# A two-layer trunk in fp32 on one core: the gate/up products at the entry of each FFN, one pair of tiles done with eight products, three pairs led, norms ahead of weights

## The chip, the core and the metric

The kernel runs on one core of a Trainium2 chip. The metric is device time of one execution in microseconds (us), as the median of several executions. Everything is computed for one sequence of 512 tokens by 1024 channels, in fp32.

## What is computed

The reference is a trunk of two layers. Each layer has a mixer and a SwiGLU FFN, and each of these sub-layers stands between two RMS norms:

```python
for layer in range(DEPTH):                      # 2
    h = rmsnorm(x, mix_pre_g[layer])
    m = even_mixer(h, ...) if layer % 2 == 0 else odd_mixer(h, ...)
    x = x + rmsnorm(m, mix_post_g[layer])
    h = rmsnorm(x, ffn_pre_g[layer])
    x = x + rmsnorm(swiglu(h, ffn_w_gate[layer], ffn_w_up[layer], ffn_w_down[layer]), ffn_post_g[layer])

def swiglu(h, w_gate, w_up, w_down):            # 512x1024 -> 512x2816 -> 512x1024
    return (jax.nn.silu(h @ w_gate) * (h @ w_up)) @ w_down
```

The change lies in the two norms ahead of `swiglu` and in its two products `h @ w_gate` and `h @ w_up`.

## The kernel before

Every fp32 product is made of three matmuls on rounded operands: each operand is split into a high and a low part, and `mm3` (L134 to L138) issues high by high (L136), low by high (L137) and high by low (L138). A split costs a cast on ACT (the high part) and a subtraction on DVE (the low part). For weights this is `split_weights`: `whi` on ACT at L158, `wlo` on DVE, which all DVE instructions record as L100 because they go through one helper.

**The gate/up products.** The 22 tiles of the hidden width are done as NP = 11 pairs of a gate and an up tile. The token axis and the contraction axis are both halved, so that a pair is a 2 by 2 block product. It is done with seven half-size products instead of eight, in the manner of Strassen and Winograd: two straight ones, A11 and A12 (tokens of blocks 0 and 1 against the two halves of the channels), four with sums of token blocks, S1 to S4, against sums of weight blocks, and A22. `gate_product` is one of these: 24 matmuls of 128x128 by 128x256. Its weight is a unit of 512 KB, loaded by SP into one of RAW = 6 `raw` buffers, in places summed in place with another (`raw<-raw` on DVE, `add_to`), then split. `first` makes A11 of a pair and copies its bank aside (L867), `second` adds A12 and gates the result (`gated`: silu on ACT at L857, a multiplication by the up tile on DVE). The rest of the pair, in the loop at the end of `ffn`, needs S1 to S4 and A22.

**The lead.** The tokens come in four blocks of 128. Blocks 0 and 1 are normed first, and A11 and A12 need only those. So the first LEAD = 5 pairs do `first` and `second` ahead of everything else, while blocks 2 and 3 are still being normed and their sums S1 to S4 are made (`Blocks.put`). `need(2, 3)` then stands ahead of the loop over the pairs.

**The norms.** `Finish` is the end of a sub-layer: `half` squares a half of an output block on ACT (L705) and multiplies it by the gain on DVE; `block` takes 1/rms (an addition on DVE, a power on POOL at L636), adds into `xres` on DVE and squares again on ACT (L722); `second` makes the normed block `h` (two `tmp<-xres,small,gain` on DVE); `transpose` makes eight transposes of it on PE (L743); then `Blocks.put` splits and sums the transposed block (casts L660, copies L668 and L672 on ACT, the rest on DVE).

**The order.** Each engine works through its queue in order. A scheduler orders the instructions of all engines by priority as the code emits them; `tc.high_priority()` moves what stands in it ahead. In the kernel before that is the splitting and summing of weights. `later(d, f)` puts a step d us of modelled work behind the present place in the stream of matmuls; T1, T2 and T3 are such delays of the norm's steps. `gate_recipes` lists the loads, sums and splits of the weight units in the order in which `unit()` hands them out.

Of the kernel before, what the change touches and what calls it, by code (L numbers as in the profile page):

```python
# [10 lines left out]
AF = mybir.ActivationFunctionType  # L11
# [8 lines left out]
NB = T // P  # L20
# [1 line left out]
FT = FF // P  # L22
NP = FT // 2

LEAD = 5
RAW = 6

A11, A12, S1, S2, S3, S4, A22 = range(7)
EPS = 1e-6
WINDOWS = (2, 4, 8, 16)  # L30
OUT_ORDER = (0, 1, 2, 7, 6, 5, 3, 4)


WARM = 8
ON_DVE = (0, 2)
# [29 lines left out]
def tile_trunk(ctx: ExitStack, tc: tile.TileContext, cst_d, sh_d, xw_d, x_d, gains_d, pw_d, w_d, out_d):  # L65
# [88 lines left out]
        return raw[:, :n]  # L154

    def split_weights(raw, hi, lo):
        with tc.high_priority():
            nc.scalar.copy(out=hi, in_=raw)  # L158
            vec.tensor_sub(out=lo, in0=raw, in1=f32(hi))

    def add_to(acc, other, eng):
        with tc.high_priority():
            eng.tensor_add(out=acc, in0=acc, in1=other)


# [15 lines left out]
    def gate_recipes(first):  # L181

        def load(j, q):
            return rawtile(w_d[first + 4 * j + q])

        for j in range(LEAD):
            recipes.append(lambda j=j: load(j, 0))
            recipes.append(lambda j=j: load(j, 3))
        for j in range(NP):
            st = {}  # L190

            def p1(j=j, st=st):
                st["v"] = load(j, 0)
                return st["v"]

            def q5(j=j, st=st):
                if j < LEAD:
                    p1(j, st)
                st["12"] = load(j, 1)
                add_to(st["v"], st["12"], vec)  # L200
                return st["v"]

            def p6(j=j, st=st):
                st["22"] = load(j, 2)
                add_to(st["v"], st["22"], vec)
                return st["v"]

            def p2(j=j, st=st):
                st["21"] = load(j, 3)
                return st["21"]  # L210

            def p7(j=j, st=st):
                add_to(st["12"], st["22"], vec)
                return st["12"]

            def q4(j=j, st=st):
# [422 lines left out]
    class Plain:  # L639


        def put(self, i, tps):
            for hf, tp in enumerate(tps):
                tv = tp.rearrange("p (k t) -> p k t", k=4)
                ks = slice(4 * hf, 4 * hf + 4)
                nc.scalar.copy(out=hBh[:, i, ks], in_=tv)
                vec.tensor_sub(out=hBl[:, i, ks], in0=tv, in1=f32(hBh[:, i, ks]))

    class Blocks:


        def put(self, i, tps):
            cs = slice(i % 2 * P, i % 2 * P + P)

            def view(ap):
                return ap.rearrange("p (k t) -> p k t", k=4)
# [12 lines left out]
                return  # L669
            ta, tb = tmp(), tmp()  # L670
            x22, s1, s2, s3 = view(ta[:, :T]), view(ta[:, T:]), view(tb[:, :T]), view(tb[:, T:])
            nc.scalar.copy(out=x22, in_=tv[1])  # L672
            vec.tensor_sub(out=s1, in0=tv[0], in1=x22)
            split(S1, s1)
            vec.tensor_sub(out=s2, in0=s1, in1=x11)
# [2 lines left out]
            split(S3, s3)  # L678
            vec.tensor_add(out=s1, in0=s2, in1=x12)
            split(S4, s1)  # L680
            split(A22, x22)

    class Finish:

# [11 lines left out]
        def half(self, i, hf, acc, made_by=None):  # L696

            if i not in self.u:
                self.u[i] = (small(2), tmp())
            ss, u = self.u[i]  # L700
            cs = slice(hf * T, (hf + 1) * T)
            if made_by is not None:
                made_by(u[:, cs])
                acc = u[:, cs]
            nc.scalar.activation(out=junk[:, cs], in_=acc, func=AF.Square, scale=1.0 / 32, accum_out=ss[:, hf:hf + 1])  # L705
            vec.tensor_mul(out=u[:, cs], in0=acc, in1=self.gpost[:, cs])

        def block(self, i):
            ss, u = self.u.pop(i)
            gpre = self.gpre  # L710
            r = rstd(ss, 2)
# [14 lines left out]
            box = {}  # L726

            def second():
                r2 = rstd(s2, len(parts))
                h = box["h"] = tmp()  # L730
                for cs in halves:
                    vec.scalar_tensor_tensor(out=h[:, cs], in0=x[:, cs], scalar=r2, in1=gpre[:, cs],
                                                   op0=ALU.mult, op1=ALU.mult)
                later(T1 if i < NB - 1 else T2, transpose)

            def transpose():
                h = box["h"]
# [92 lines left out]
    def ffn(layer):  # L830
# [30 lines left out]
        def first(j):  # L861

            b1 = ps()
            gate_product(b1, unit(), A11)

            y = gs[NP - 1 - j][:, 1] if j < LEAD else ytile()
            nc.scalar.copy(out=y, in_=b1)  # L867
            return b1, y

        def second(j, b1):  # L870
            gate_product(b1, unit(), A12, True)
            gated(j, 0, b1, tmp()[:, :256])

        led = []
        need(0, 1)
        for j in range(LEAD):
            led.append(first(j))
            second(j, led[j][0])
        need(2, 3)
        for j in range(NP):  # L880
            b1, y = led[j] if j < LEAD else first(j)
            z, c = hx[:, j % 2, :T], hx[:, j % 2, T:]
            b3 = ps()
            gate_product(b3, unit(), S1)
# [233 lines left out]
```

## Time and profile before

| | |
|---|---|
| median of 3 runs | 1083.9 us (1083.37 to 1085.91) |
| the profiled execution | 1087.36 us |
| its span in the trace | 1085.6 us |
| PE busy | 1041.1 us (96%) |
| PE weight loads busy | 931.0 us (86%) |
| DVE busy | 768.8 us (71%) |
| ACT busy | 516.9 us (48%) |
| mean granted clock of PE | 0.988 |

PE is TensorE's matmuls, PEld its weight loads, which run beside them, DVE is VectorE, ACT ScalarE, POOL GpSimd, SP the queue that issues the loads. The busy time of PE is modelled from pipelined matmuls, so a busy PE is not PE at its peak. The two FFNs are called FFN 0 and FFN 1 below. The gate/up stage of FFN 0 runs from its first matmul on `hTh` at 196.74 us to the first matmul of the down product at 434.01 us, that of FFN 1 from 722.67 to 957.08 us.

### The profile page before, as it was taken

How to read it: one execution, taken by the hardware profiler on the slowest of the kernel's cores; microseconds unless marked ns; L12 is line 12 of the kernel's file. 1: busy time of each engine (PE TensorE's matmuls, PEld its weight loads, DVE VectorE, ACT ScalarE, POOL GpSimd, SP SyncE). 2: the span in 40 equal slices, each digit the busy share in tenths (PEclk: the TensorE clock that was granted, in tenths of full speed). 3: DMA queues.
4: the chain of work that ended last, by engine and by line, in shares of the span. 5: the costliest groups of instructions: out<-in, count | busy, mean ns of one | idle time of the engine just before them, and what ended most of it. 6: DMA issues, size and time to landing. Idle time of an engine off the chain costs nothing. (4 is left out here: it accounts for less than half of the span.)

```text
span 1085.6 us, 16315 instructions
## 1 busy us (share of the span) xinstructions
PE 1041.1 (96%) x6558; PEld 931.0 (86%) x6558; DVE 768.8 (71%) x1045; ACT 516.9 (48%) x815; POOL 60.7 (6%) x96
## 2 busy tenths in 40 slices
PE   8989999789999999999999999897999999999997
PEld 6867777789999999888898887687999999988886
DVE  3778875788998989432357589468899889963313
ACT  6747644654444446332245894355444444542301
POOL 0020100100000000000012102210000000000000
PEclk9989999899999999999999999998999999999999
DMA  8563353232443244334123234132442432443201
GB/s 320 170 146 83 107 171 120 98 114 101 156 131 104 80 139 131 113 108 150 57 75 101 84 110 152 26 115 97 148 141 101 129 105 80 136 135 98 98 1 77
DMA packets 36188, 125.08 MB, mean 115 GB/s; under 512 B 4368, under 2 KB 4368, under 8 KB 36112
## 3 DMA queue, kind: packets, MB, share of 16 engines
q1 hardware_dynamic: 35536, 121.94, 35.6%
q10 hardware_dynamic: 576, 2.10, 0.5%
q8 instruction: 51, 0.84, 0.3%
q14 instruction: 25, 0.20, 0.1%
HBM read 117.73 MB, written 2.10 MB: 110 GB/s over the span
## 5 line engine op out<-in xcount | busy, mean ns | idle before, releaser
L158 ACT CAST whi<-raw 128x1024 fp32r<-128x1024 f32 x230 | 239.0, 1047 | 310.4 <-PE ps L137 113.1
L100 DVE TENSOR_TENSOR wlo<-raw,whi 128x1024 fp32r<-128x1024 f32 (+1 forms) x238 | 286.3, 1212 | 124.7 <-ACT whi L158 119.6
L136 PE MATMUL ps<-hTh,whi 128*128 128x256 f32 (+1 forms) x960 | 294.6, 307 | 5.5 <-ACT whi L158 2.5
L138 PE MATMUL ps<-hTh,wlo 128*128 128x256 f32 (+1 forms) x960 | 294.0, 307 | 3.8 <-DVE wlo L100 3.8
L137 PE MATMUL ps<-hTl,whi 128*128 128x256 f32 (+1 forms) x960 | 292.2, 305 | 3.5 <-DVE hTl L100 3.5
L136 PEld LDWEIGHTS ps<-hTh,whi 128*128 128x128 f32 x960 | 182.7, 190 | 15.0 <-ACT whi L158 3.1
L138 PEld LDWEIGHTS ps<-hTh,wlo 128*128 128x128 f32 x960 | 182.4, 190 | 13.3 <-DVE wlo L100 4.6
L137 PEld LDWEIGHTS ps<-hTl,whi 128*128 128x128 f32 x960 | 182.8, 190 | 12.2 <-DVE hTl L100 3.7
L136 PE MATMUL ps<-up,whi 128*128 128x256 f32 x528 | 149.8, 284 | 2.2 <-DVE hx L100 2.1
L137 PE MATMUL ps<-up,whi 128*128 128x256 f32 x528 | 149.4, 283 | 0.0
L138 PE MATMUL ps<-up,wlo 128*128 128x256 f32 x528 | 149.2, 283 | 0.0
L100 DVE TENSOR_TENSOR raw<-raw 128x1024 f32<-128x1024 f32 x88 | 106.9, 1220 | 8.1 <-DMA raw<-in_w 7.8
L136 PEld LDWEIGHTS ps<-up,whi 128*128 128x128 f32 x528 | 101.1, 191 | 3.1 <-DVE hx L100 3.0
L137 PEld LDWEIGHTS ps<-up,whi 128*128 128x128 f32 x528 | 101.2, 192 | 0.0
L138 PEld LDWEIGHTS ps<-up,wlo 128*128 128x128 f32 x528 | 101.1, 192 | 0.0
L100 DVE TENSOR_TENSOR tmp<-ps,gain 128x512 f32<-128x512 f32 x32 | 21.9, 690 | 59.0 <-ACT junk L705 58.9
L636 POOL TENSOR_TENSOR small<-small,nhalf 128x1 f32<-128x1 f32 x28 | 15.4, 549 | 800.1 <-DVE small L100 800.1
L137 PE MATMUL ps<-wlo,hTh 128*128 128x512 f32 (+2 forms) x160 | 55.8, 352 | 3.2 <-DVE wlo L100 3.1
L138 PE MATMUL ps<-whi,hTl 128*128 128x512 f32 (+2 forms) x160 | 55.5, 350 | 0.0
L136 PE MATMUL ps<-whi,hTh 128*128 128x512 f32 (+2 forms) x160 | 54.3, 351 | 0.6 <-ACT whi L303 0.6
L705 ACT ACTIVATE junk<-ps 128x512 bf16<-128x512 f32 x32 | 19.0, 596 | 60.7 <-PE ps L138 60.2
L138 PE MATMUL ps<-whi,hTh 128*128 128x512 f32 x96 | 38.0, 396 | 0.0
(220 smaller groups left out, 1655.3 us busy)
## 6 DMA issues: line engine op xcount, KB each, us to landing
raw<-in_w SPq DMA_DIRECT2D x200, 512.0 KB, 3.8
gain<-in_gains SPq DMA_DIRECT2D x7, 512.0 KB, 4.2
raw<-in_xw SPq DMA_DIRECT2D x6, 516.0 KB, 9.1
big<-in_x ACTq DMA_DIRECT2D x4, 512.0 KB, 7.8
big<-big SPq DMA_DIRECT2D x16, 128.0 KB, 4.2
xres<-in_x SPq DMA_DIRECT2D x4, 512.0 KB, 5.0
out_dram<-xres SPq DMA_DIRECT2D x3, 512.0 KB, 2.6
big<-tmp SPq DMA_DIRECT2D x8, 128.0 KB, 3.9
```

The lines of the kernel that those rows point to most:

```text
L100: self.last = fn(*a, **k)
L136: nc.tensor.matmul(out, lhsT=ah, rhs=bh, start=start, stop=False, skip_group_check=more)
L137: nc.tensor.matmul(out, lhsT=ah, rhs=bl, start=False, stop=False, skip_group_check=more)
L138: nc.tensor.matmul(out, lhsT=al, rhs=bh, start=False, stop=stop, skip_group_check=more)
L158: nc.scalar.copy(out=hi, in_=raw)
L636: nc.gpsimd.tensor_tensor(out=r, in0=ms, in1=nhalf[:, :1], op=ALU.pow)
L705: nc.scalar.activation(out=junk[:, cs], in_=acc, func=AF.Square, scale=1.0 / 32, accum_out=ss[:, hf:hf + 1])
```

## The change

One pair (number 3, `WHOLE`) is done with all eight block products, A11, A12, A21 and A22, straight on the four quarters of its weights: each weight unit is used twice, and no weight sums, bank adds or copies are made for it. It comes right behind the leads, and the leads are three pairs instead of five. A21, the lower token half against the first half of the channels, is split straight from the transposes into a new slot, and A22 too, ahead of the sums. The norm's steps are issued in high priority, the weights' splits and sums in `high_priority(AHEAD)`, and the transposes of this norm 2.5 us of modelled work later.

```diff
-LEAD = 5
+LEAD = 3
+
+WHOLE = LEAD
...
+AHEAD = 1500
...
     def split_weights(raw, hi, lo):
-        with tc.high_priority():
+        with tc.high_priority(AHEAD):
...
     def add_to(acc, other, eng):
-        with tc.high_priority():
+        with tc.high_priority(AHEAD):
...
+        for q in (0, 3, 1, 2):
+            recipes.append(lambda q=q: load(WHOLE, q))
         for j in range(NP):
+            if j == WHOLE:
+                continue
...
     class Blocks:
...
+        delay = 2.5
...
+            split(A21, tv[0])
             nc.scalar.copy(out=x22, in_=tv[1])
+            split(A22, tv[1])
...
-            split(A22, x22)
...
-            nc.scalar.activation(out=junk[:, cs], in_=acc, func=AF.Square, scale=1.0 / 32, accum_out=ss[:, hf:hf + 1])
-            vec.tensor_mul(out=u[:, cs], in0=acc, in1=self.gpost[:, cs])
+            with tc.high_priority():
+                nc.scalar.activation(out=junk[:, cs], in_=acc, func=AF.Square, scale=1.0 / 32,
+                                     accum_out=ss[:, hf:hf + 1])
+                vec.tensor_mul(out=u[:, cs], in0=acc, in1=self.gpost[:, cs])
 
         def block(self, i):
+            with tc.high_priority():
+                self._block(i)
...
-                later(T1 if i < NB - 1 else T2, transpose)
+                later((T1 if i < NB - 1 else T2) + self.sink.delay, transpose)
...
         for j in range(LEAD):
-            led.append(first(j))
-            second(j, led[j][0])
-        need(2, 3)
+            b1 = first(j)
+
+            nc.scalar.copy(out=gs[NP - 1 - j][:, 1], in_=b1)
+            second(j, b1)
+        ws = [unit(), unit()]
+        for n in range(2):
+            for f, fs in ((2 * n, (A11, A12)), (2 * n + 1, (A21, A22))):
+                b = ps()
+                if f == 1:
+                    need(2, 3)
+                gate_product(b, ws[0], fs[0])
+                gate_product(b, ws[1], fs[1], True)
+                gated(WHOLE, f, b, tmp()[:, :256])
+            if n == 0:
+                ws = [unit(), unit()]
         for j in range(NP):
-            b1, y = led[j] if j < LEAD else first(j)
+            if j == WHOLE:
+                continue
```

Lines of the changed kernel are shifted: DVE's L100 is L104, `whi` L162, the squares L719 and L741, the transposes L763, the silu L877, the copy of a led bank L895.

How the order of work moves is shown at three places, all at the entry of FFN 0. The first is DVE, from the addition behind the square of block 2 to the normed block 3. In the rows `xres_1831` is block 2 of the stream, `xres_1833` block 3, `wlo` the low part of a weight, and `tmp<-xres,small,gain` the normed block `h`. Before:

```order
L100 TENSOR_SCALAR small_2108<-small_2077 128x1
L100 TENSOR_TENSOR tmp_2093<-ps_1948,gain_1823 128x512
L100 SCALAR_TENSOR_TENSOR tmp_2112<-xres_1831,small_2110,gain_1825 128x512
L100 TENSOR_TENSOR wlo_2205<-raw_2206,whi_2204 128x1024
L100 SCALAR_TENSOR_TENSOR tmp_2112<-xres_1831,small_2110,gain_1825 128x512
L100 TENSOR_TENSOR tmp_2093<-ps_1949,gain_1823 128x512
L100 SCALAR_TENSOR_TENSOR small_2117<-small_2092 128x1
L100 SCALAR_TENSOR_TENSOR xres_1833<-tmp_2093,small_2119,xres_1833 128x512 x2
L100 TENSOR_TENSOR wlo_2263<-raw_2264,whi_2262 128x1024
L100 TENSOR_TENSOR wlo_2324<-raw_2325,whi_2323 128x1024
L100 SCALAR_TENSOR_TENSOR small_2190<-small_2121 128x1
L100 SCALAR_TENSOR_TENSOR tmp_2194<-xres_1833,small_2192,gain_1825 128x512 x2
```

The same stretch in the changed kernel:

```order
L104 TENSOR_SCALAR small_2108<-small_2077 128x1
L104 TENSOR_TENSOR tmp_2093<-ps_1948,gain_1823 128x512
L104 SCALAR_TENSOR_TENSOR small_2117<-small_2092 128x1
L104 TENSOR_TENSOR tmp_2093<-ps_1949,gain_1823 128x512
L104 SCALAR_TENSOR_TENSOR tmp_2112<-xres_1831,small_2110,gain_1825 128x512
L104 SCALAR_TENSOR_TENSOR xres_1833<-tmp_2093,small_2119,xres_1833 128x512
L104 SCALAR_TENSOR_TENSOR tmp_2112<-xres_1831,small_2110,gain_1825 128x512
L104 SCALAR_TENSOR_TENSOR xres_1833<-tmp_2093,small_2119,xres_1833 128x512
L104 TENSOR_TENSOR wlo_2205<-raw_2206,whi_2204 128x1024
L104 SCALAR_TENSOR_TENSOR small_2190<-small_2121 128x1
L104 SCALAR_TENSOR_TENSOR tmp_2194<-xres_1833,small_2192,gain_1825 128x512 x2
```

Of the three low parts that stood between the norms one is left, and the addition for block 3 (`small_2117`) goes ahead of the gain multiplication of its second half.

The second place is ACT in the same stretch, from the square of block 2 to the copy of the first banks; `junk<-xres` are the squares, `whi` the high parts of weights. Before:

```order
L722 ACTIVATE junk_68,small_2077<-xres_1831 128x1024
L705 ACTIVATE junk_68,small_2092<-ps_1948 128x512
L158 CAST whi_2204<-raw_2206 128x1024
L705 ACTIVATE junk_68,small_2092<-ps_1949 128x512
L867 COPY g_2142<-ps_2143 128x512
L722 ACTIVATE junk_68,small_2121<-xres_1833 128x512
L158 CAST whi_2262<-raw_2264 128x1024
L158 CAST whi_2323<-raw_2325 128x1024
L722 ACTIVATE junk_68,small_2121<-xres_1833 128x512
L857 ACT_TABLE_LOAD
```

And in the changed kernel:

```order
L719 ACTIVATE junk_68,small_2092<-ps_1948 128x512
L719 ACTIVATE junk_68,small_2092<-ps_1949 128x512
L680 COPY hx_67<-ps_2051 128x4x128
L162 CAST whi_2204<-raw_2206 128x1024
L895 COPY g_2142<-ps_2143 128x512
L741 ACTIVATE junk_68,small_2121<-xres_1833 128x512 x2
L162 CAST whi_2264<-raw_2266 128x1024
L877 ACT_TABLE_LOAD
L877 ACTIVATE tmp_2200<-ps_2143 128x256
L162 CAST whi_2298<-raw_2300 128x1024
L672 CAST up0_2130<-ps_2234 128x4x128
```

The two high parts that parted the squares of block 3 now stand behind them, and the next high part but one stands behind the table load and the first silu.

The third is PE, around the transposes of block 3 (`tmp_2194`); `ps_2143`, `ps_2203` and `ps_2297` are the banks of the first, second and third led pair. Before:

```order
L743 MATMUL ps_2218<-ident_70,tmp_2112 128x128 x4
L137 MATMUL ps_2203<-hTl_66,whi_2015 128x256
L138 MATMUL ps_2203<-hTh_65,wlo_2016 128x256
L136 MATMUL ps_2203<-hTh_65,whi_2015 128x256
L137 MATMUL ps_2203<-hTl_66,whi_2015 128x256
L138 MATMUL ps_2203<-hTh_65,wlo_2016 128x256
L743 MATMUL ps_2280<-ident_70,tmp_2194 128x128 x4
L743 MATMUL ps_2285<-ident_70,tmp_2194 128x128 x4
L136 MATMUL ps_2203<-hTh_65,whi_2021 128x256
```

And in the changed kernel:

```order
L763 MATMUL ps_2234<-ident_70,tmp_2112 128x128 x4
L763 MATMUL ps_2239<-ident_70,tmp_2112 128x128 x4
L140 MATMUL ps_2297<-hTh_65,whi_2204 128x256
L141 MATMUL ps_2297<-hTl_66,whi_2204 128x256
L142 MATMUL ps_2297<-hTh_65,wlo_2205 128x256
L140 MATMUL ps_2297<-hTh_65,whi_2204 128x256
L141 MATMUL ps_2297<-hTl_66,whi_2204 128x256
L142 MATMUL ps_2297<-hTh_65,wlo_2205 128x256
L140 MATMUL ps_2297<-hTh_65,whi_2204 128x256
L141 MATMUL ps_2297<-hTl_66,whi_2204 128x256
L142 MATMUL ps_2297<-hTh_65,wlo_2205 128x256
L763 MATMUL ps_2313<-ident_70,tmp_2194 128x128 x4
```

The transposes of block 3 stood 72 matmuls behind the stage's first, and now stand 81 behind it; the product that follows them adds into `ps_2203` before, and belongs to the third pair now, `ps_2203` being taken up 96 matmuls behind the first.

## Rows read from the trace of the kernel before

**Rows 1.** The page, part 1: busy time of each engine.

```profile
PE 1041.1 (96%) x6558; PEld 931.0 (86%) x6558; DVE 768.8 (71%) x1045; ACT 516.9 (48%) x815; POOL 60.7 (6%) x96
```

**Rows 2.** Timeline of PE, FFN 0: start, length, instruction, [idle before].

```profile
196.74 0.28 PE L136 MATMUL ps<-hTh,whi 128*128 128x256 f32 x1
...
211.86 1.94 PE L743 MATMUL ps<-ident,tmp 128*128 128x128 f32 x8 [4.94 <-DVE tmp L100]
...
289.03 0.38 PE L136 MATMUL ps<-up,whi 128*128 128x256 f32 x1 [0.78 <-DVE hx L100]
...
434.01 0.40 PE L136 MATMUL ps<-whi,up 128*128 128x512 f32 x1
```

**Rows 3.** Timeline of PE, FFN 1.

```profile
722.67 0.28 PE L136 MATMUL ps<-hTh,whi 128*128 128x256 f32 x1
...
733.40 1.04 PE L743 MATMUL ps<-ident,tmp 128*128 128x128 f32 x8
734.20 0.37 PE L136 MATMUL ps<-hTh,whi 128*128 128x256 f32 x1
...
821.79 0.39 PE L136 MATMUL ps<-up,whi 128*128 128x256 f32 x1 [0.77 <-DVE hx L100]
...
957.08 0.40 PE L136 MATMUL ps<-whi,up 128*128 128x512 f32 x1
```

**Rows 4.** Waits of PE in 196.7 to 434 us: total, times, longest.

```profile
PE ps L743 <- DVE tmp L100: 5.3, 2, 4.9
PE ps L136 <- ACT whi L158: 2.5, 3, 1.1
PE ps L138 <- DVE wlo L100: 2.3, 3, 0.8
PE ps L136 <- DVE hx L100: 1.3, 2, 0.8
```

**Rows 5.** Waits of PE in 722.6 to 957 us.

```profile
PE ps L137 <- DVE hTl L100: 3.5, 1, 3.5
PE ps L136 <- ACT hTh L660: 2.1, 1, 2.1
PE ps L138 <- DVE wlo L100: 1.5, 1, 1.5
PE ps L743 <- DVE tmp L100: 1.3, 1, 1.3
PE ps L136 <- DVE hx L100: 0.8, 1, 0.8
```

**Rows 6.** Windows: stretch, us, busy PE, PEld, DVE, ACT, POOL, then PEclk, DMA, GB/s.

```profile
212.00:217.00 5.00, 5.00 (x27) 5.00 (x28) 4.75 (x7) 1.69 (x4) 0.00 (x0) 0.56 0.56 219
...
743.00:754.00 11.00, 4.00 (x29) 3.39 (x28) 11.00 (x14) 3.88 (x6) 0.00 (x0) 0.92 0.42 143
754.00:760.00 6.00, 6.00 (x32) 6.00 (x33) 4.31 (x9) 3.35 (x5) 0.00 (x0) 0.57 0.00 0
```

**Rows 7.** Timeline of DVE, FFN 0, around the norm of block 3.

```profile
202.06 1.22 DVE L100 TENSOR_TENSOR wlo<-raw,whi 128x1024 fp32r<-128x1024 f32 x1
...
207.87 2.36 DVE L100 TENSOR_TENSOR wlo<-raw,whi 128x1024 fp32r<-128x1024 f32 x2 [1.11 <-ACT whi L158]
...
210.96 1.42 DVE L100 SCALAR_TENSOR_TENSOR tmp<-xres,small,gain 128x512 f32<-128x512 f32 x2 [0.66 <-POOL small L636]
```

**Rows 8.** Timeline of ACT, FFN 0.

```profile
209.42 1.28 ACT L857 ACT_TABLE_LOAD   x1
```

**Rows 9.** Groups by line, FFN 0, 196.7 to 434 us: count | busy, mean ns.

```profile
L100 DVE TENSOR_TENSOR wlo<-raw,whi 128x1024 fp32r<-128x1024 f32 x76 | 91.7, 1220 | 15.0 <-ACT whi L158 11.7 <-PE ps L138 3.1
L158 ACT CAST whi<-raw 128x1024 fp32r<-128x1024 f32 x76 | 78.6, 1048 | 101.9 <-PE ps L137 47.8 <-DVE raw L100 40.5 <-issue 10.4
L100 DVE TENSOR_TENSOR raw<-raw 128x1024 f32<-128x1024 f32 x44 | 53.4, 1220 | 3.9 <-DMA raw<-in_w 3.7
...
L867 ACT COPY g<-ps 128x512 f32<-128x512 f32 x5 | 2.9, 585 | 0.0
```

More of the change, by code (lines that the diff above doesn't have):

```diff
@@ L23 @@
 NP = FT // 2
-LEAD = 5
+LEAD = 3
+WHOLE = LEAD
 RAW = 6
-A11, A12, S1, S2, S3, S4, A22 = range(7)
+A11, A12, S1, S2, S3, S4, A22, A21 = range(8)
 EPS = 1e-6
@@ L639, in tile_trunk @@
     class Plain:
+        delay = 0.0
         def put(self, i, tps):
@@ L704, in half, with _block @@
                 acc = u[:, cs]
-            nc.scalar.activation(out=junk[:, cs], in_=acc, func=AF.Square, scale=1.0 / 32, accum_out=ss[:, hf:hf + 1])
-            vec.tensor_mul(out=u[:, cs], in0=acc, in1=self.gpost[:, cs])
+            with tc.high_priority():
+                nc.scalar.activation(out=junk[:, cs], in_=acc, func=AF.Square, scale=1.0 / 32,
+                                     accum_out=ss[:, hf:hf + 1])
+                vec.tensor_mul(out=u[:, cs], in0=acc, in1=self.gpost[:, cs])
         def block(self, i):
+            with tc.high_priority():
+                self._block(i)
+        def _block(self, i):
             ss, u = self.u.pop(i)
@@ L728, in second @@
             def second():
[L729 to L733, printed above, removed]
-                later(T1 if i < NB - 1 else T2, transpose)
+                with tc.high_priority():
+                    r2 = rstd(s2, len(parts))
+                    h = box["h"] = tmp()
+                    for cs in halves:
+                        vec.scalar_tensor_tensor(out=h[:, cs], in0=x[:, cs], scalar=r2, in1=gpre[:, cs],
+                                                       op0=ALU.mult, op1=ALU.mult)
+                later((T1 if i < NB - 1 else T2) + self.sink.delay, transpose)
             def transpose():
@@ L864, in first @@
             gate_product(b1, unit(), A11)
-            y = gs[NP - 1 - j][:, 1] if j < LEAD else ytile()
-            nc.scalar.copy(out=y, in_=b1)
-            return b1, y
+            return b1
         def second(j, b1):
@@ L872, in second @@
             gated(j, 0, b1, tmp()[:, :256])
-        led = []
         need(0, 1)
         for j in range(LEAD):
-            led.append(first(j))
-            second(j, led[j][0])
-        need(2, 3)
-        for j in range(NP):
-            b1, y = led[j] if j < LEAD else first(j)
+            b1 = first(j)
[12 more added lines that the diff above has]
+                ws = [unit(), unit()]
+        for j in range(NP):
+            if j == WHOLE:
+                continue
+            if j < LEAD:
+                y = gs[NP - 1 - j][:, 1]
+            else:
+                b1 = first(j)
+                y = ytile()
+                nc.scalar.copy(out=y, in_=b1)
             z, c = hx[:, j % 2, :T], hx[:, j % 2, T:]
```

## The prediction

> **What bounds the kernel now.** The page's first part comes first: PE is busy 96% of the span, DVE 71%, ACT 48% [rows 1]. By that PE is the bound, and a change that adds products to it could only lose. But this is a mean over stages, so I look at PE's own timeline in the two stages that the change touches. The gate/up stage of FFN 0 runs from 196.74 to 434.01 us, 237.3 us [rows 2]; that of FFN 1 from 722.67 to 957.08, 234.4 us [rows 3]. The trace has 1848 matmuls in each (77 products of 24) and 16 transposes. What would they take without a wait? Behind 289.03 us PE never waits again in FFN 0: 1218 matmuls in 145.0 us, 0.119 us each [rows 2]. In FFN 1 it is 1138 in 135.3 us behind 821.79, the same [rows 3]. Eight transposes take 0.80 us (733.40 to 734.20) [rows 3]. So a stage without waits is 1848 x 0.119 + 1.6 = 221.5 us, and the lost time is 15.8 us in FFN 0 and 12.9 in FFN 1, **28.7 us** together. All of it lies ahead of 290 and of 822 us.
>
> The waits say what it is lost to. In FFN 0: 5.3 us for a normed block (`tmp`, one wait of 4.94 at 211.86), 4.8 for weight parts, 1.3 for banks; 11.4 in all [rows 2, 4]. In FFN 1: 5.6 us for the casts of transposed blocks, 1.5 for `wlo`, 1.3 for a normed block, 0.8 for banks; 9.2 [rows 5]. Behind the long waits the granted clock is low: 0.56 in 212 to 217 us and 0.57 in 754 to 760, near the lower of its two levels (1.2 of 2.4 GHz) [rows 6]. There 19 matmuls and 8 transposes took 5 us instead of 3.1, and 32 matmuls 6 us instead of 3.8: 4.1 us. Waits and clock are 24.7 of the 28.7 us; 4.0 are spread in pieces that I can't name.
>
> Who is late? In 743 to 754 us DVE is busy 11.00 of 11 us while PE does 4.00 [rows 6]. And in FFN 0 the normed block 3 ends at 212.4 us because a `wlo` of 1.22 us and two of 2.36 together stand between the steps of its norm [rows 7]. At both entries the bound is DVE, and the order in which it works.
>
> **What the change removes.** For each FFN the order takes from DVE three `wlo` and four sums of weights, 1.22 us each [rows 9], and five bank additions, and adds two half-block splits, about half a `wlo` each: some 10 us less DVE work. ACT loses three `whi` of 1.05 us and a copy and gains two casts, about 2.5 us less. SP's queue has four weight loads less in each FFN; their waits are small (3.7 us of DVE's idle time in FFN 0 ended by a load) [rows 9].
>
> The norm of block 3 loses two of the three `wlo` on DVE and both `whi` between its squares on ACT. Two `wlo`, the 1.11 us wait for them on ACT, and part of the third are 2.4 + 1.1 + 1.2 = 4.7 us; squares that are no longer parted, and an addition that no longer waits, give some 2 more. So `h` of block 3 ends near 206 us instead of 212.4. PE reaches its transposes 81 matmuls and 8 transposes behind the first matmul: 196.7 + 9.6 + 0.8 = 207.1 us. The 4.94 us wait goes, with its low clock. In FFN 1 the same count gives about 733, and `h` about 731.
>
> PE then has 14 products (3 pairs led, 8 of the whole pair) ahead of the first that needs a sum, instead of 10. That is 40 us, against 28.6. A21 of block 3, which is needed at about the tenth product, is cast straight from the transposes. The two late casts of FFN 1, 5.6 us [rows 5], go by this: the sums have 11 us more, and DVE makes four `wlo` for eight products in that time.
>
> **What it adds.** One product more in each FFN, on the engine that sets the time: 2 x 24 x 0.119 = **5.7 us**, at the price measured in these same stages [rows 2, 3]. The Trainium skill ("TensorE: Matmul & The Clock Gate", section Back-to-back issue gap) gives N/2.4 + 2.5 ns for a matmul at the upper clock level; by that estimate 256 columns are 109 ns, the term 5.2 and the total 0.5 us less. The rows show 119 and decide.
>
> **What is late next.** First, the weights, which now stand behind the norms. On ACT two `whi`, the table load of 1.28 us [rows 8], a silu and three casts or copies of about 0.6 stand between the squares of block 3 (end near 204.7) and the copy of the second led bank; with the copy itself some 6.2 us, so at latest 210.9. PE adds into that bank 96 matmuls and 16 transposes behind the first, at 209.7. That is a wait between 0 and 1.2 us. I take 0.7, for this copy and again for that of the third bank: 1.4 an entry, **2.8** in all. Second, the led pairs: each needs five `wlo` and four sums for five products, 9 x 1.22 us and its bank work against 14.3 us of PE. Before, five such pairs cost the hx waits (1.3 and 0.8) and about a third of the 4.8 us for weight parts; three pairs keep three fifths, with some margin **3.0** for both FFNs. Third, of the 4.0 unnamed us I keep half, **2.0** (the ends are 0 and 4).
>
> **Edits at nothing.** The table loads stay where a silu first wants them. POOL has only the powers of the norms here, in the same sequence. The later transposes (2.5 us of modelled work) cost PE nothing, since it has led products there; without them it would stand. At the very end the order puts the 1/rms of the last block ahead of a gain multiplication, half a `wlo` in size: **0.6 us** less, in a tail that nothing covers. Entries of the mixers: the order shows little, 0 to 1 us either way.
>
> **The sum.** 28.7 - (2.8 + 3.0 + 2.0) - 5.7 + 0.6 = 15.8 us saved. The profiled execution has a span of 1085.6 us and its own time is 1087.36, 1.8 above; so 1069.8 of span, 1071.6 of time. The median stands 3.5 us under that execution: **1068 us**.
>
> **Bounds.** If only 1 us of waits is left in each FFN, 28.7 - 2 - 5.7 + 0.6 = 21.6: 1062. If the named remainders are twice as large, 15.6 instead of 7.8, it is 1076.
>
> **Rivals.**
> *A long wait stays at an entry* (0.20). For it: ACT's queue at the entry is long, the copies of the led banks and the casts of A21 stand in it, and PE takes its queue in order. Against it: ACT is 48% busy, and A21 has some 2 us of slack. One wait of the size that the rows show, 3.5 to 4.9, with the 1.9 to 2.2 us of low clock behind it, is 5.4 to 7.1: about 1074 if in one FFN (0.14), about 1081 if in both (0.06).
>
> *The stall is only moved, and the kernel is slower* (0.07). Its place is the transposes of block 3, at about 207 us as before. PE stands there, in order, until `h` is made. Before, DVE made two `wlo` in that wait; now these come behind the norm. If the chain of block 3 (a square, a power on POOL, two additions, again squares) is bound by its own handovers, `h` comes hardly sooner, the wait stays, and the weights are late behind it. It decides at 28.7 - 5.7 + 0.6 = 23.6 us: if more than that of the 28.7 stays, the change loses, and with all of it the time is 1083.9 + 5.7 - 0.6 = 1089. Against it: the rows of DVE's chain are full of weight work. The Trainium skill ("Perfetto Trace Analysis", section Identifying the Most-Contended Engine) would have the engine of highest occupancy improved first, and TensorE judged by its weight loads' busy share; by that PE, with 86% of weight loads against DVE's 71%, is the one not to load further, and the time would be about 1089 as well. The rows of 743 to 754 us speak against it in these stages: PE 4.00 of 11, DVE 11.00.
>
> *It does less than it says* (0.02): the order shows the products and the norms moved, so I give this almost nothing; about 1084. *Almost no wait stays* (0.03): 1062.
>
> **How the numbers follow.** The forecast has 0.68, with a range of its own of 1062 to 1075. Leaving out both long waits (0.06), the slower case (0.07), the unchanged one and some of each edge, the range is 1061 to 1078. A measurement of this kernel tells about 0.3%, 3.3 us, from no change. Faster by more: the forecast, the better case, one long wait, and a third of two: 0.87. Within 0.3%: 0.06. Slower: 0.07.
>
> **What would show it.** Right: the stages are 224 to 231 us long; no wait of PE above 2 us ahead of 300 and 825 us; no window with a clock near 0.56 there; the transposes of block 3 without a wait; `h` of block 3 near 206 us. The steady 0.119 us stays. Wrong: a wait for a cast, a copy of a led bank or `whi` above 3 us, or `h` of block 3 still near 212.

## The result and the profile after

The changed kernel takes 1065.6 us (median of 4 runs, 1063.9 to 1067.1) against 1084.9 before (4 runs, 1083.4 to 1086.3): a ratio of 0.9822, 95% interval 0.980 to 0.9844. That is 19.3 us less, where 15.8 were forecast. Time 1065.6 lies in the range of 1061 to 1078.

The profiled execution of the changed kernel took 1063.9 us, its span is 1062.1, the lowest of its four; that of the kernel before (1087.4) lies above all four of its runs. So the two profiles differ by 23.5 us, more than the medians. Cut at the first matmul on `hTh` of each gate/up stage and at the first of each down product:

| stretch | before | after | difference |
|---|---|---|---|
| start to the gate/up stage of FFN 0 | 196.7 | 191.2 | -5.5 |
| gate/up stage of FFN 0 | 237.3 | 227.1 | -10.2 |
| from there to that of FFN 1 | 288.7 | 288.4 | -0.3 |
| gate/up stage of FFN 1 | 234.4 | 226.1 | -8.3 |
| down product of FFN 1 | 121.4 | 121.4 | 0.0 |
| from the last matmul's start to the end | 7.1 | 7.9 | +0.8 |

The two stages give 18.5 us. Of the 5.5 us at the start 5.0 are not the change's: they are there at the first square of the norm ahead of FFN 0 (180.14 us before, 175.15 after), and up to it PE, DVE and ACT have the same instructions in the same order in both kernels. PE's timeline in that stretch, of the kernel before:

```profile
60.21 0.88 PE L529 MATMUL ps<-big 128*128 128x256 f32 x4 [1.83 <-DMA big<-tmp]
64.29 0.55 PE L530 MATMUL ps<-big 128*128 128x256 f32 x1 [2.73 <-issue]
```

and of the changed kernel:

```profile
58.07 0.89 PE L537 MATMUL ps<-big 128*128 128x256 f32 x4 [0.72 <-DMA big<-tmp]
61.35 0.35 PE L538 MATMUL ps<-big 128*128 128x256 f32 x1 [1.93 <-DVE wlo L104]
```

The same matmuls come 2.1 and then 2.9 us sooner; the first of them waits for `big<-tmp` transfers, which landed at 59.97 and 60.51 us before and at 57.82 and 58.42 after. In 60 to 80 us the granted clock is 0.83 before and 1.00 after. In the profiled executions of the fourteen kernels named below that first square starts anywhere from 174.6 to 180.1 us, with the same order of instructions ahead of it in all of them, and the stage of FFN 0 begins anywhere from 190.7 to 196.7. I therefore read each kernel by its two stages as well as by its time.

Page, part 1, changed kernel, which answers to [rows 1]:

```profile
PE 1038.0 (98%) x6606; PEld 930.0 (88%) x6606; DVE 751.0 (71%) x1025; ACT 510.5 (48%) x811; POOL 65.6 (6%) x96
```

PE has 48 matmuls more, one product in each FFN, and yet 3 us less busy time: in the kernel before, matmuls at a low clock were long (19 matmuls and 8 transposes in 5.00 us at 0.56 [rows 6]). DVE has 17.8 us less work in all.

Timeline of PE, FFN 0 of the changed kernel (start, length, instruction; it answers to [rows 2]):

```profile
191.22 0.40 PE L140 MATMUL ps<-hTh,whi 128*128 128x256 f32 x2
...
201.82 1.04 PE L763 MATMUL ps<-ident,tmp 128*128 128x128 f32 x8
...
418.29 0.40 PE L140 MATMUL ps<-whi,up 128*128 128x512 f32 x1
```

The transposes of block 3, which waited 4.94 us, now wait for nothing. Waits of PE in 191 to 418.2 us, which answers to [rows 4]:

```profile
PE ps L140 <- ACT g L895: 1.1, 2, 0.9
PE ps L142 <- DVE wlo L104: 0.7, 1, 0.7
```

and in 706.5 to 932.7 us, FFN 1, which answers to [rows 5]:

```profile
PE ps L140 <- ACT g L895: 0.8, 3, 0.3
PE ps L140 <- DVE hx L104: 0.4, 1, 0.4
```

Of 20.6 us of waits 3.0 are left, none above 0.9. Windows of the changed kernel (columns as in [rows 6]):

```profile
207.00:217.00 10.00, 8.42 (x70) 8.02 (x69) 10.00 (x14) 5.80 (x10) 0.00 (x0) 1.00 0.31 112
217.00:227.00 10.00, 10.00 (x87) 10.00 (x86) 9.95 (x14) 6.24 (x11) 0.00 (x0) 1.00 0.15 54
...
728.00:743.00 15.00, 14.71 (x124) 14.50 (x123) 14.40 (x23) 9.45 (x16) 0.00 (x0) 1.00 0.23 76
```

The granted clock is full in all three. DVE is still busy for 19.95 of 20 us in FFN 0, but PE works beside it: 8.42 and 10.00 of 10 us. DVE's load at the entry hasn't gone; it is covered.

A stage of 78 products (1872 matmuls) without a wait would be 1872 x 0.119 + 1.6 = 224.4 us, by the prediction's rate. So 2.7 and 1.7 us are lost now, 4.4 us instead of 28.7.

### The profile page after: what moved, and what is told of

Its sections match the earlier page's. It is cut to its first block, busy times and chain, and to the rows that moved or that the text cites. A ratio compares the mean times of both kernels' runs of the same rounds, so it can differ in the third digit from the quotient of the medians.

```text
span 1062.1 us, 16378 instructions
## 1 busy us (share of the span) xinstructions
PE 1038.0 (98%) x6606; PEld 930.0 (88%) x6606; DVE 751.0 (71%) x1025; ACT 510.5 (48%) x811; POOL 65.6 (6%) x96
## 5 line engine op out<-in xcount | busy, mean ns | idle before, releaser
L162 ACT CAST whi<-raw 128x1024 fp32r<-128x1024 f32 x224 | 232.8, 1048 | 304.6 <-PE ps L141 93.8
L104 DVE TENSOR_TENSOR wlo<-raw,whi 128x1024 fp32r<-128x1024 f32 (+1 forms) x232 | 279.6, 1213 | 132.1 <-ACT whi L162 129.5
L142 PEld LDWEIGHTS ps<-hTh,wlo 128*128 128x128 f32 x960 | 180.1, 188 | 9.4 <-DVE wlo L104 0.9
L140 PE MATMUL ps<-up,whi 128*128 128x256 f32 x544 | 154.1, 283 | 0.5 <-DVE hx L104 0.4
L141 PE MATMUL ps<-up,whi 128*128 128x256 f32 x544 | 153.9, 283 | 0.0
L142 PE MATMUL ps<-up,wlo 128*128 128x256 f32 x544 | 153.9, 283 | 0.0
L140 PEld LDWEIGHTS ps<-up,whi 128*128 128x128 f32 x544 | 104.2, 192 | 0.9 <-issue 0.9
L142 PEld LDWEIGHTS ps<-up,wlo 128*128 128x128 f32 x544 | 104.3, 192 | 0.0
L141 PEld LDWEIGHTS ps<-up,whi 128*128 128x128 f32 x544 | 104.3, 192 | 0.0
L104 DVE TENSOR_TENSOR raw<-raw 128x1024 f32<-128x1024 f32 x80 | 97.2, 1219 | 2.8 <-issue 1.9
L719 ACT ACTIVATE junk<-ps 128x512 bf16<-128x512 f32 x32 | 19.0, 597 | 62.3 <-PE ps L142 62.0
L104 DVE TENSOR_TENSOR tmp<-ps,gain 128x512 f32<-128x512 f32 x32 | 21.9, 688 | 37.9 <-ACT junk L719 37.9
```

The costliest lines, as they stand in the source:

```text
L104: self.last = fn(*a, **k)
L140: nc.tensor.matmul(out, lhsT=ah, rhs=bh, start=start, stop=False, skip_group_check=more)
L141: nc.tensor.matmul(out, lhsT=ah, rhs=bl, start=False, stop=False, skip_group_check=more)
L142: nc.tensor.matmul(out, lhsT=al, rhs=bh, start=False, stop=stop, skip_group_check=more)
```

## The experiments

All but later_only have the changed kernel as their base; later_only has the kernel before. The sums of the two stages, from each kernel's profiled execution, stand beside its time. The times were taken at several occasions, with the kernel before run at each (medians of 1084.8 to 1087.3), and the ratio is to its runs of the same occasion; so the ratios compare better than the medians.

| kernel | stages, us | median, us | ratio to before, 95% interval |
|---|---|---|---|
| before | 237.3 + 234.4 = 471.7 | 1084.9 | |
| changed | 227.1 + 226.1 = 453.2 | 1065.6 | 0.9822 [0.980, 0.9844] |
| order_only | 232.1 + 232.1 = 464.2 | 1078.5 | 0.9923 [0.9897, 0.9949] |
| whole_only | 226.6 + 227.3 = 453.9 | 1067.3 | 0.9826 [0.9798, 0.9855] |
| no_later | 226.5 + 227.2 = 453.7 | 1068.9 | 0.9823 [0.9786, 0.9861] |
| three_led_no_whole | 234.9 + 232.8 = 467.7 | 1080.1 | 0.9936 [0.9914, 0.9959] |
| later_only | 234.2 + 234.9 = 469.1 | 1081.4 | 0.995 [0.9932, 0.9968] |
| no_reuse | 225.1 + 227.2 = 452.3 | 1064.4 | 0.9802 [0.9768, 0.9837] |
| lead1 | 225.9 + 225.2 = 451.1 | 1064.6 | 0.9798 [0.9768, 0.9828] |
| order_copy | 233.0 + 230.0 = 463.1 | 1072.9 | 0.9883 [0.9854, 0.9911] |
| lead1_no_reuse | 232.4 + 233.6 = 466.0 | 1080.7 | 0.9953 [0.993, 0.9976] |
| two_whole | 227.9 + 228.5 = 456.5 | 1069.5 | 0.9856 [0.983, 0.9881] |
| pool_low | 233.3 + 232.7 = 466.0 | 1079.8 | 0.9951 [0.9931, 0.9972] |
| lead2_copy | 225.8 + 226.1 = 451.9 | 1063.2 | 0.9788 [0.9763, 0.9813] |

**The order of work alone: order_only.** Five pairs led, no whole pair; norms first and later transposes, as in the changed kernel.

```diff
-LEAD = 3
-WHOLE = LEAD
+LEAD = 5
+WHOLE = -1
...
-        for q in (0, 3, 1, 2):
-            recipes.append(lambda q=q: load(WHOLE, q))
...
-            split(A21, tv[0])
             nc.scalar.copy(out=x22, in_=tv[1])
-            split(A22, tv[1])
...
+            split(A22, x22)
...
-        ws = [unit(), unit()]
...
+        need(2, 3)
```

> The changed kernel without its whole pair: five pairs led as before, 77 products, but norms ahead of weights and the later transposes. Theory A (the lost time came mostly from the order of work on DVE and ACT at the entry): the normed block 3 is made some 9 us behind the stage's first matmul, no wait of 5 us for it, no window of low clock behind it; the sums are wanted after 10 products, near 32 us, and are made near 31 to 34, so 0 to 3 us of wait there. Stages of 224 to 228 us, 1061 to 1068 us. Rival B (DVE simply has too much work, and the whole pair's relief is what pays): a wait of 3 us or more for a cast stays in each FFN with low clock behind it, stages of 231 us and more, 1074 us and more.

Neither: 464.2 us, a gain of 7.5. The wait for block 3 went, as theory A had it, but others came three to five products later. PE's timeline of order_only:

```profile
220.53 0.39 PE L140 MATMUL ps<-hTh,whi 128*128 128x256 f32 x1 [2.51 <-ACT g L892]
...
226.42 0.39 PE L140 MATMUL ps<-hTh,whi 128*128 128x256 f32 x1 [1.44 <-ACT hTh L670]
...
227.76 0.39 PE L141 MATMUL ps<-hTl,whi 128*128 128x256 f32 x1 [0.96 <-DVE hTl L104]
```

and its windows there:

```profile
217.00:232.00 15.00, 10.09 (x57) 9.39 (x56) 13.27 (x18) 6.04 (x10) 0.00 (x0) 0.77 0.33 99
```

The first wait is for the copy of a led bank, the others for the high and low part of the first sum. They make 4.9 us, with a low clock behind them (a mean of 0.77 over these 15 us). In FFN 1 the same waits make 5.0. With norms first, the weights and sums are what is late.

DVE is not alone in this. ACT's timeline of order_only, and one row of DVE's:

```profile
217.94 1.04 ACT L162 CAST whi<-raw 128x1024 fp32r<-128x1024 f32 x1 [2.81 <-PE ps L141]
...
224.80 1.04 ACT L162 CAST whi<-raw 128x1024 fp32r<-128x1024 f32 x1 [3.80 <-PE ps L141]
225.75 0.61 ACT L670 CAST hTh<-tmp 128x512 fp32r<-128x512 f32 x1
```

```profile
223.04 0.68 DVE L104 TENSOR_TENSOR tmp<-ps,tmp 128x512 f32<-128x512 f32 x1
```

DVE has the first sum ready at 223.7 us, but its cast stands on ACT behind a `whi` that waited 3.80 us for PE to be done with an older product, and starts at 225.75. So part of these waits is the order of ACT's queue. No run was made with those two casts the other way round, or with more than the four weight tiles of each kind.

**The whole pair alone: whole_only.** Priorities as before, the later transposes kept.

```diff
-        with tc.high_priority(AHEAD):
+        with tc.high_priority():
...
-            with tc.high_priority():
-                nc.scalar.activation(out=junk[:, cs], in_=acc, func=AF.Square, scale=1.0 / 32,
...
-            with tc.high_priority():
-                self._block(i)
+            self._block(i)
...
```

> The changed kernel with the order of priorities of before: three pairs led and the whole pair, later transposes, weights ahead of norms. Theory A: the normed block 3 is as late as before, near 15.6 us behind the first matmul, and its transposes stand 96 matmuls behind it, at 13.0 us, so a wait of 2 to 3 us in FFN 0 stays; the waits for casts in FFN 1 go, because the sums have 11 us more. Stages near 229 to 231, 1070 to 1075 us. Rival B (the relief is what pays): as fast as the changed kernel, 1064 to 1067 us.

Rival B: 453.9 us against the changed kernel's 453.2, and times whose intervals lie on each other. The two profiles differ by 0.7 us in the stages, too little to tell: beside the whole pair and the later transposes the priorities bring nothing that shows. PE's wait for block 3 in FFN 0 of whole_only:

```profile
206.78 1.23 PE L760 MATMUL ps<-ident,tmp 128*128 128x128 f32 x8 [1.01 <-DVE tmp L104]
```

and DVE ahead of it:

```profile
202.72 2.42 DVE L104 TENSOR_TENSOR wlo<-raw,whi 128x1024 fp32r<-128x1024 f32 x2
...
205.88 1.42 DVE L104 SCALAR_TENSOR_TENSOR tmp<-xres,small,gain 128x512 f32<-128x512 f32 x2
```

The two `wlo` still stand in the norm of block 3, which ends at 207.3, 14.5 us behind the first matmul (15.6 before). The transposes stand 24 matmuls (2.9 us) later than in the kernel before, by the delay that this run keeps (later_only, with the delay and no whole pair, has them 22 later), and 1.0 us is all that is left of 4.94. The whole pair with neither the norms' order nor the delay was not run; by these rows some 3.9 us of that wait would stay in FFN 0 (an estimate: 1.0 + 2.9).

**The later transposes: no_later and later_only.** The first puts `delay = 0.0` for `Blocks` in the changed kernel; the second is the kernel before with 2.5.

```diff
-        delay = 2.5
+        delay = 0.0
```

> The changed kernel with its transposes not put later (0 instead of 2.5 us of modelled work). Those of block 2 then stand 33 matmuls behind the first, at 3.9 us, while that block is made near 5.2 us: a wait of about 1.3 us in each FFN, 1068 to 1069 us by theory A. If the later transposes matter as much as the rest: 1072 us and more. If something else hides them: 1065.6 us.

The stages took 453.7 us, 0.5 more than with the delay; the median of 1068.9 is the one that theory A names, but over runs from 1062.6 to 1070.0, and the ratio is that of the changed kernel. The waits for transposes come to 0.8 us, one in FFN 1 and none in FFN 0; theory A's 1.3 us in each aren't there. Block 3's transposes in FFN 0 stand 72 matmuls behind the first here, as in the kernel before, and wait for nothing: for the 4.94 us wait the norms' order is enough without the delay.

> The kernel before with one edit: its transposes ahead of the FFNs put 2.5 us of modelled work later, so that block 3's stand 94 matmuls behind the first instead of 72. Five pairs led, no whole pair, weights ahead of norms. The wait for block 3 in FFN 0 (4.94 us) shrinks to 2 or 3 us, and its low clock may go. Theory C (the length of the lead decides: 14 products or 10 before the first sum is wanted): the sums are as late as before, the waits for casts in FFN 1 stay or grow; stages together 465 to 471 us, 1076 to 1084 us. Theory F (the later transposes alone do what the whole pair seemed to do): stages together 455 to 460 us, 1066 to 1072 us.

Theory C by the numbers: 469.1 us, a gain of 2.6. The wait for block 3 shrank to 1.29 us, and 2.51, 1.54 and 1.21 us of waits for a copy and the first sum follow it. Neither the delay alone nor the delay with the norms' order does what the whole pair does.

**Fewer products ahead: three_led_no_whole.** As order_only, with `LEAD = 3`.

> The changed order with three pairs led and no whole pair: six products, 17 us, ahead of the first that needs a sum, 77 products. The sums are made some 29 us behind the first matmul. Theory A: a wait of 6 to 10 us in each FFN for the sums, with 2 us of low clock behind it, less one product of 2.9: stages of 231 to 238 us, 1074 to 1088 us. If the sums could be made sooner when nothing else is in the way, less: stages near 226, 1064 us.

As theory A had it. Waits of PE in FFN 0, and then in FFN 1:

```profile
PE ps L140 <- ACT g L892: 9.3, 2, 9.1
```

```profile
PE ps L140 <- ACT g L892: 8.3, 3, 7.3
```

In each stage PE stands for 7 to 9 us, ahead of its sixth product. What it waits for is the copy of a led bank; on ACT that copy stands behind casts of sums, which wait for DVE:

```profile
218.82 1.22 ACT L670 CAST up<-tmp 128x512 fp32r<-128x512 f32 x2 [3.44 <-DVE tmp L104]
```

The whole pair is what PE does in that time.

**Length or relief: no_reuse and lead1.** The whole pair does two things at once: it puts products ahead of the first sum, and it uses each split unit twice. no_reuse takes the second away, lead1 the first.

```diff
-        for q in (0, 3, 1, 2):
+        for q in (0, 3, 0, 3, 1, 2, 1, 2):
             recipes.append(lambda q=q: load(WHOLE, q))
...
-        ws = [unit(), unit()]
         for n in range(2):
             for f, fs in ((2 * n, (A11, A12)), (2 * n + 1, (A21, A22))):
+                ws = [unit(), unit()]
...
-            if n == 0:
-                ws = [unit(), unit()]
```

> The changed kernel with the four units of its whole pair loaded and split anew for each second use: four loads, four casts on ACT and four subtractions of 1.2 us on DVE more in each FFN, ahead of the first sum; the lead is 14 products as in the changed kernel. Theory C (length of the lead): at most 1 us more in each stage, stages together 453 to 456 us, 1065 to 1069 us. Theory D (the relief: units used twice keep DVE free while the sums are made): the waits for the casts of the sums come back, stages together 460 us or more, 1072 us or more.

```diff
-LEAD = 3
+LEAD = 1
```

> The changed kernel with one pair led instead of three: 10 products (6 units of weights) ahead of the first that needs a sum, as many as in the kernel before (10 units). Theory C: sums are wanted 32 us behind the first matmul, where they aren't ready; waits of 2 to 5 us in each FFN, stages together 460 us or more, 1072 us or more. Theory D: six units instead of ten leave DVE 5 us for the sums, so no wait beyond those of the changed kernel, stages together 452 to 455 us, 1064 to 1067 us.

Both theories fell, each as the only cause. no_reuse has 452.3 us, against D; lead1 has 451.1, against C. Either half is enough. So I formed a third, an account: the products ahead must last as long as DVE's and ACT's work there. Four products more with four units more give 4 x (2.86 - 1.22) = 6.5 us of room, four units less 4 x 1.22 = 4.9; and order_only had lacked 4.9 and 5.0. (The numbers are estimates, from 24 x 0.119 us a product and 1.22 us a `wlo`.)

**Neither: lead1_no_reuse.** Both edits at once.

> One pair led and a whole pair whose units are loaded and split anew for each use: 10 products and 10 units of weights ahead of the first sum, as many as in the kernel before, with norms ahead of weights. Theory E (an account: the lead must last as long as DVE's and ACT's work ahead of the first sum; five pairs led fall some 5 us short; four more products with four more units add 6.5 us, four units less add 4.9 us, and either is enough): with neither, the waits of some 5 us come back in each FFN, beside the product more; stages together 464 to 470 us, 1076 to 1084 us. Theory G (something else in the whole pair helps, as A21 and A22 being split ahead of the sums): stages together 451 to 456 us, 1063 to 1068 us.

466.0 us, as theory E had it; G, at 451 to 456, is out. PE's timeline of lead1_no_reuse, in FFN 0 and in FFN 1:

```profile
219.24 0.58 PE L141 MATMUL ps<-up,whi 128*128 128x256 f32 x1 [5.31 <-DVE up L104]
...
741.54 0.52 PE L141 MATMUL ps<-up,whi 128*128 128x256 f32 x1 [3.74 <-DVE up L104]
```

DVE just ahead of the first:

```profile
218.50 1.28 DVE L104 TENSOR_TENSOR up<-ps,up 128x512 fp32r<-128x512 f32 x2
```

With 0.8 and 1.8 us waited for a cast just before, this is 6.1 and 5.5 us: near the size that the account gives. The place is another one than I had expected. What is late is the low part of A21 and A22 of block 3, wanted after six products, and not a sum. The same two subtractions in lead1:

```profile
213.66 1.28 DVE L104 TENSOR_TENSOR up<-ps,up 128x512 fp32r<-128x512 f32 x2
```

There they start 18.4 us behind the stage's first matmul (195.27), and DVE makes two `wlo` in that stretch; in lead1_no_reuse they start 24.9 us behind it (193.62), with six `wlo` and two sums of weights ahead of them. That is 7.3 us of weights more, for low parts that come 6.5 us later. So the account holds as one of DVE's work ahead of the first product that isn't ready on blocks 2 and 3, whichever that is. How much of the waits is due to the order of ACT's queue, as in order_only, stays open.

**The price of a product: two_whole.**

```diff
-WHOLE = LEAD
+WHOLES = tuple(range(LEAD, LEAD + 2))
```

(with the loads, the loop over the whole pairs and the two tests on `WHOLE` written for the tuple).

> The changed kernel with a second whole pair behind the first: one more product in each FFN, and less work on DVE. No wait above 1 us is left to remove, so this measures the price of a product: 2 x 2.86 = 5.7 us on the two stages, less at most 1 us of bank waits; stages together 457.5 to 459 us, 1069 to 1072 us. If the work taken from DVE still paid: under 456 us, 1068 us.

456.5 us, 3.3 more than the changed kernel, under the forecast of 4.3 to 5.8. Waits of PE in the stage of FFN 0, and then of FFN 1:

```profile
PE ps L140 <- DVE hx L104: 0.2, 1, 0.2
PE ps L140 <- ACT g L896: 0.2, 1, 0.2
```

```profile
PE ps L140 <- DVE hx L104: 0.5, 1, 0.5
PE ps L140 <- ACT g L896: 0.5, 2, 0.3
```

A stage of 79 products without waits is 1896 x 0.119 + 1.6 = 227.2 us, so 2.0 us are lost in both, 2.4 less than in the changed kernel: 5.7 - 2.4 = 3.3. This agrees with the price, but doesn't measure it apart from the rate of 0.119, which stands on both sides; PE's waits, counted by themselves, fell from 3.0 to 1.4 us. The relief still gave something back. Each of the four runs (1068.8 to 1070.0) is above all four of the changed kernel, but the intervals of the ratios overlap, so the kernel is likely slower than the changed one, and not shown to be.

**Room without the product: pool_low and order_copy.** By the account 5 us of DVE's work taken elsewhere should serve with 77 products. pool_low is order_only with

```diff
-                vec.tensor_sub(out=lo, in0=src, in1=f32(hi))
+                eng = nc.gpsimd if f in (S2, S3, S4, A22) else vec
+                eng.tensor_sub(out=lo, in0=src, in1=f32(hi))
```

> Five pairs led, no whole pair (77 products), norms ahead of weights, and the low parts of S2, S3, S4 and A22 made on POOL instead of DVE: 8 subtractions of 0.6 us each leave DVE in each FFN, 4.8 us, at about 1.5 us each on POOL. By theory E this closes the 5 us: waits of 0 to 2 us in each FFN without the product more; stages together 446 to 452 us, 1057 to 1063 us. If POOL is too slow in the chain, or slows DVE, waits of 3 us and more for its low parts: 458 us and more, 1070 us and more.

466.0 us, a failure, and not by POOL's own lateness. DVE's timeline of pool_low:

```profile
220.60 0.68 DVE L104 TENSOR_TENSOR tmp<-hx,ps 128x512 f32<-128x512 f32 x1
221.20 0.69 DVE L104 TENSOR_TENSOR tmp<-tmp,hx 128x512 f32<-128x512 f32 x1
221.80 1.80 DVE L104 TENSOR_TENSOR hTl<-tmp,hTh 128x512 fp32r<-128x512 f32 x1
223.63 1.66 DVE L104 TENSOR_TENSOR tmp<-tmp,hx 128x512 f32<-128x512 f32 x1
225.21 2.28 DVE L104 TENSOR_TENSOR raw<-raw 128x1024 f32<-128x1024 f32 x1
227.42 2.31 DVE L104 TENSOR_TENSOR wlo<-raw,whi 128x1024 fp32r<-128x1024 f32 x1
```

and POOL's at the same time:

```profile
219.35 5.39 POOL L672 TENSOR_TENSOR up<-tmp,up 128x512 fp32r<-128x512 f32 x3 [3.56 <-ACT up L670]
224.69 1.72 POOL L672 TENSOR_TENSOR hTl<-tmp,hTh 128x512 fp32r<-128x512 f32 x1
226.37 2.28 POOL L672 TENSOR_TENSOR up<-tmp,up 128x512 fp32r<-128x512 f32 x1
```

While POOL works, most of DVE's instructions take longer: 2.3 us instead of 1.22, and 1.7 to 1.8 instead of 0.68. PE then waits for `wlo`: 4.78 and 2.38 us in FFN 0. What left DVE came back as longer instructions, so this says nothing on the account.

order_copy is order_only with the copies of led banks in high priority.

```diff
+            with tc.high_priority():
                 nc.scalar.copy(out=gs[NP - 1 - j][:, 1], in_=b1)
             second(j, b1)
```

> Norms ahead of weights without a whole pair, as in the run before of that kind, and the copies of the led banks in high priority on ACT. There each FFN waited 2.5 us for such a copy, behind casts that wait for DVE. If the copy itself is what is late, 5 us less: stages together near 459 us, 1073 us. If the copy only shows that DVE is late with the sums, the wait turns up at the casts: stages together 462 to 465 us, 1076 to 1079 us.

This is not settled: the median of 1072.9 is the first case, the stages of 463.1 (of an execution that was the slowest of its runs) the second. In them the waits for copies shrank from 2.51 to 1.5 us, and those for the cast behind grew from 1.4 and 1.5 to 2.0 and 1.8. The changed kernel is ahead of it either way: the intervals of the ratios don't overlap.

**Two pairs led, copies first: lead2_copy.** The edit of order_copy on the changed kernel, with `LEAD = 2`.

> The changed kernel with two pairs led instead of three, and the copies of the led banks in high priority on ACT: 12 products and 8 units ahead of the first sum, between the run with one pair led and the changed kernel, both of which had 1 to 3 us of waits in each stage. By theory E the lead is long enough (margin near 6 us), and the waits for the copies, 0.2 to 0.9 us each, go: stages together 450 to 452 us, 1062 to 1065 us. If the copies ahead of whi make the weights late instead: 454 us and more, 1066 us and more.

451.9 us and 1063.2, as forecast: 2.1% under the kernel before. Its interval overlaps that of the changed kernel, so it is not shown to be faster than that one.

## Why the prediction was right, and where its reasons were not

The time fell as forecast, and 3.5 us further, and nearly each sign that was to show it was there: stages of 227.1 and 226.1 us (224 to 231 said), no wait above 2 us, a granted clock of 1.00 over both stages, the transposes of block 3 without a wait, and that block made soon. The sum came out because it took all of the lost time away and asked only what would be left; which part of the change took it away didn't enter, and there the reasons were only half right. DVE's timeline of the changed kernel, which answers to [rows 7]:

```profile
198.74 1.42 DVE L104 SCALAR_TENSOR_TENSOR tmp<-xres,small,gain 128x512 f32<-128x512 f32 x2 [0.67 <-POOL small L644]
...
200.08 1.22 DVE L104 TENSOR_TENSOR wlo<-raw,whi 128x1024 fp32r<-128x1024 f32 x1
```

It ends at 200.2 us, 8.9 behind the stage's first matmul, where 9.3 were worked out ("near 206" less 196.7).

*The lost time, 28.7 us.* Right: all of it lay ahead of the pairs that need no lead, and 24.3 us of it came back. The kernel now loses 4.4.

*The product more, 5.7 us.* Right as far as the runs show. The rate that it was priced by holds after the change: a stretch of each stage without a wait has 1349 and 1350 matmuls in 160 us, 0.119 us each.

```profile
255.00:415.00 160.00, 160.00 (x1349) 1.00 0.35 114
770.00:930.00 160.00, 160.00 (x1350) 1.00 0.36 114
```

(These windows are of PE alone: stretch, us, busy PE, PEclk, DMA, GB/s.) two_whole agrees, by the same rate.

*What is late next, 7.8 us.* Mis-sized; it measured 4.4. What stands behind the norms cost 2.6 us instead of 2.8: 1.9 for copies of led banks, and 0.7 for a `wlo`, which I hadn't named. The led pairs cost 0.4 for banks instead of 3.0; the unnamed rest is 1.4 instead of 2.0. These 3.4 us are what the stages beat the sum by (18.5 against 28.7 - 7.8 - 5.7 = 15.2).

*The end.* Right: from the start of the last matmul to the end of the last addition into `xres` it is 4.1 us before and 3.5 after. The output's last transfer behind it took 3.2 us in the profiled execution, against 2.0 before, so the span doesn't show it.

*"The 4.94 us wait goes" because the norm loses two `wlo`.* Right for the wait, and wrong for what it is worth. In no_later the norm is sooner, the transposes stand where they stood, and the wait is gone. But the gain didn't hang on it: in whole_only the two `wlo` stay in the norm, the later transposes leave 1.0 us of the wait, and the stages are as short. And where the wait was gone and the whole pair missing, order_only, waits of 4.9 us came behind it and more than half of the gain was not there. I had counted the norms' order as a gain by itself, while without the whole pair it mostly chooses what is late first. The whole pair is what gives DVE room; with that room either the norms' order or the later transposes will do for block 3.

*"PE then has 14 products ... instead of 10".* Half a reason. 14 products are enough without reuse (no_reuse), 10 are enough with it (lead1), and only without both (lead1_no_reuse) do the waits return. The 10 was wrong as well: the scheduler puts the first product with a sum ahead of the last led ones, so that by the count of matmuls it comes after seven products in FFN 1 of the kernel before (the wait for a cast at 749.94 us), after eight in order_only, and after 14 in the changed kernel (235.44 us). There PE starts on A21 of block 3 after some eight (219.21 us), but A21 needs no sum. The reason that fits the runs best is the account of DVE's work against PE's, to which the text came closest in "the sums have 11 us more, and DVE makes four `wlo` for eight products in that time". The text also took the later transposes to be needed ("without them it would stand"): without them PE stands 0.8 us, in FFN 1.

*The rivals.* A long wait at an entry is what happened wherever the whole pair was missing (longest waits of 2.5 to 9.1 us; 2.0 with the copies first). The stall that is only moved is order_only's case: the wait for block 3 turned into waits of nearly the same sum some products later. It didn't make that kernel slower, since it has no product more. In lead1_no_reuse, which has one, the ratio is 0.9953: hardly any gain, and not slower. The rule of the Trainium skill ("Perfetto Trace Analysis", Identifying the Most-Contended Engine), to improve the engine of highest occupancy first, points at PE when it is read on the whole span. That more work on PE must lose was the prediction's own step from there, and the runs contradict that step: 5.7 us more of matmuls, and a kernel 19.3 us faster. Read on the stretch in which PE stood and DVE was busy, the same rule points at DVE, which is where the relief went.

## What to carry to other kernels

Where a stage begins with work that another engine has yet to prepare, count both sides up to the first instruction that needs it: how long the lead lasts, and how much the preparing engine has to do in that time, weights included. If the second is larger, reordering it moves most of the wait from one operand to the next, as order_only shows; what helped here was more work of the bound engine ahead of that instruction, or less for the preparing one. Here 5.7 us of such work, with the new order, bought back 24.3. And test the parts of such a change one by one: two of them may each be enough, so that taking away either shows nothing.

## What was not expected

Two things of the chip. First, POOL and DVE slowed one another. In pool_low most of DVE's subtractions and additions on two operands in SBUF that ran beside POOL took 1.66 to 2.32 us where 0.68 and 1.22 are usual, while those with an operand in PSUM, as `tmp<-hx,ps` at 220.60, kept their 0.68 (five of them beside a POOL that worked all the while). Not each of the first kind was slowed: `tmp<-tmp,hx` at 221.20, and in FFN 1 two in a row at 744.66 and 745.27, kept 0.68 as one of POOL's instructions ended and the next began (which then took 1.83 and 2.45 us), and two `wlo` of 1.2 us overlapped POOL for 0.73. The shortest of POOL's own in these stages was 1.30. The Trainium skill ("SBUF — State Buffer", Who interferes with whom) has it so: a DVE instruction with two SBUF inputs contends with a GpSimd instruction that reads SBUF, one with at most one such input doesn't. The runs agree with the second half in every row, and with the first in most. An idle POOL is no free place for DVE's work of this kind.

Second, the stretch up to the first square ahead of FFN 0 took from 174.6 to 180.1 us in the fourteen profiled executions, with the same order of instructions in all of them. So one profile of each kernel can't tell a change of that size by its span; stages cut at the same instructions can.
